# Spreading the conditioning row by DMA, taking both inverse roots in one chain, and splitting the first feature group into single blocks

## The chip, the cores and the metric

The kernel runs on one core of one Trainium2 chip. A core has a matrix engine (TensorE, PE in the tables), a vector engine (VectorE, DVE), a scalar engine (ScalarE, ACT), GpSimd (POOL) and SyncE (SP); each works through its own list of instructions strictly in order, and 16 DMA engines move data between HBM and the on-chip memory (SBUF). Matmul results land in a second on-chip memory, PSUM. The metric is the time of one execution in microseconds, as the device measures it.

## The reference

Two layers on 256 tokens of 1024 features. All is fp32. Cut to what matters here:

```
c_act = silu(c)                                   # c: one row of 1024
for l in range(2):
    mod = c_act @ w_ada[l] + b_ada[l]             # six vectors of 1024
    sh_a, sc_a, g_a, sh_f, sc_f, g_f = mod
    u = rmsnorm(x, attn_norm[l]) * (1 + sc_a) + sh_a
    y = token_mixer(u, w_in[l], ...)              # three branches, gates, w_out
    x = x + g_a * y
    hf = rmsnorm(x, ffn_norm[l]) * (1 + sc_f) + sh_f
    x = x + g_f * hier_moe(hf, ...)               # 16 experts, top 2 of one group
```

`u @ w_in` is the first matmul of a layer. Its input needs `rmsnorm(x)` and the first two vectors of `mod`, which need `silu(c)` and a third of `w_ada`.

## The kernel before

The change touches only the start of layer 0, up to the first three column chunks of `w_in` (called first, second and third chunk: 424, 512 and 512 columns).

**Conditioning row.** `c` (one row) is loaded into one partition; a matmul with a column of ones spreads it over 128 partitions into PSUM, in two halves of 512 (L266); ACT takes tanh (L267) and DVE makes `cb`, twice silu (L268).

**Norm.** `normed(t)` runs for the two blocks of 128 tokens: two squares with row sums on ACT (L439), then ten small DVE instructions (L440, L441 and the eight of `rsqrt`, L114 to L123), then two scalings on ACT into `xn` (L445).

**Groups of features.** The 1024 input features are eight blocks of 128, taken in four groups of two. For a group, DVE multiplies four half-megabyte pieces of `w_ada` with `cb` and sums along the row (`matvec`, L284, 128x1024 each); `modulation` adds bias and gain (L289, L292); ACT applies them to the transposed `xn` (L564, one per block) and rounds the result to the matmul type, `uh` (L565); DVE makes the rest, `ul` (L566). Each piece of `w_in` is split likewise: ACT makes `h` (L579), DVE makes `lo` (L580), both in one of four rotating buffers (`rs.get`, `rs.put`: rs_85 to rs_88). A buffer can be written again only when the matmuls that read it have ended. PE then multiplies `uh` by `h`, `ul` by `h` and `uh` by `lo` (`mm3`, L474 to L476; `second_chunk`, L503 to L505). Transposes of `xn` for the next group are issued a group ahead (`turned`, L546).

**Loads.** SP issues the list `loads` in order; up to eight transfers are in flight, and a transfer waits where its buffer is not yet free. Within a group the `w_ada` pieces stand ahead of the three `w_in` pieces. The order in which each engine runs its instructions is fixed when the program is built, by a scheduler: an instruction that waits holds all that is behind it on its engine.

Of the kernel before, what the change touches and what calls it, by code (L numbers as in the profile page):

```python
# [19 lines left out]
F32 = mybir.dt.float32  # L20
F32R = mybir.dt.float32r
I32 = mybir.dt.int32
AF = mybir.ActivationFunctionType
OP = mybir.AluOpType
# [3 lines left out]
L, D, S = 2, 1024, 256  # L28
EPS = 1e-6
# [42 lines left out]
def tile_block(ctx: ExitStack, tc: tile.TileContext, x_in, c_in, cst_in, sv_in, aux_in, wada_in, ws_in, out, depth=L):  # L72
    nc = tc.nc
    PE, DVE, ACT, POOL, SP = nc.tensor, nc.vector, nc.scalar, nc.gpsimd, nc.sync
# [4 lines left out]
    work = ctx.enter_context(tc.tile_pool(name="work", bufs=2))  # L79
# [17 lines left out]
    def mmt(name="mm"):  # L97
        return psum.tile([128, 512], F32, name=name)
# [3 lines left out]
    cb = persist.tile([128, D], F32, name="cb")  # L102
    x = fs.get().rearrange("p (t d) -> p t d", t=2)
    svs = [persist.tile([128, N_SV], F32, name=f"sv{l}") for l in range(depth)]
    ones = persist.tile([128, 128], F32, name="ones")
# [5 lines left out]
    def rsqrt(y, ms, n):  # L111

        t = work.tile([128, 64], F32, name="nt")[:, :n]
        DVE.tensor_scalar(y.bitcast(I32), ms.bitcast(I32), -0.5, 1597463007.0, op0=OP.mult, op1=OP.add)  # L114
        DVE.tensor_tensor(t, y, y, op=OP.mult)
        DVE.scalar_tensor_tensor(t, t, -0.5, ms, op0=OP.mult, op1=OP.mult)
        DVE.scalar_tensor_tensor(y, t, 1.5, y, op0=OP.add, op1=OP.mult)

        c = 0.375 ** 0.5
        DVE.tensor_tensor(t, y, y, op=OP.mult)  # L120
        DVE.scalar_tensor_tensor(t, t, c, ms, op0=OP.mult, op1=OP.mult)
        DVE.scalar_tensor_tensor(t, t, -1.25 / c, t, op0=OP.add, op1=OP.mult)
        DVE.scalar_tensor_tensor(y, t, 1.875, y, op0=OP.add, op1=OP.mult)  # L123
# [19 lines left out]
    halves = [slice(512 * hf, 512 * hf + 512) for hf in range(2)]  # L143
# [11 lines left out]
    for l in range(depth):  # L155
        w_order[l] += list(range(6, nd)) + [nd + i for i in expert_order]

    groups = [(0, 2), (2, 4), (4, 6), (6, 8)]
    for k0, k1 in groups:
        loads += [("b", 0, (i, k)) for k in range(k0, k1) for i in (k // 2, 4 + k // 2)]  # L160
        loads += [("p", 0, (2 * j + k0 // 4, k0 % 4, (k1 - 1) % 4 + 1)) for j in range(3)]
# [41 lines left out]
    def pump(most=len(loads)):  # L203

        for _ in range(most):
            if nxt[0] == len(loads):
                return
            kind, l, i = key = loads[nxt[0]]
            if kind == "u":
                if len(fs.free) < 2:  # L210
                    return
                t = [(fs, fs.get()), (fs, fs.get())]
                SP.dma_start(t[0][1][:, :1536], aux_in[l, :, :1536])
                SP.dma_start(t[1][1][:, :1024], aux_in[l, :, 1536:2560])
                SP.dma_start(wr, aux_in[l, :, 2560:])
            elif kind in "bp" and (i[1] % 2 if kind == "b" else i[1]):
                dst, src = part(kind, i)
                SP.dma_start(dst, src)
                loaded[key] = None
                nxt[0] += 1  # L220
                continue
            else:
                if wa.free:
                    t = (wa, wa.get())
                elif len(fs.free) > keep():
                    t = (fs, fs.get())
                elif lend[0] and rs.free and l == cur[0]:
                    t = (rs, rs.get(F32))
                else:
                    return  # L230
                if kind == "a":
                    SP.dma_start(t[1], wada_in[l, i])
                elif kind in "bp":
                    raws[kind, i[0]] = t
                    dst, src = part(kind, i)
                    SP.dma_start(dst, src)
                    t = None
                elif i < 2:
                    SP.dma_start(t[1][:, :4 * A0], ws_in[l, i, :, :4 * A0])
                else:  # L240
                    SP.dma_start(t[1], ws_in[l, i])
            loaded[key] = t
            nxt[0] += 1
# [8 lines left out]


    tmp_s = fs.get()
    tmp = tmp_s[:, :1024]
    crow = tmp_s[:1, 1024:]
    SP.dma_start(crow, c_in)
    SP.dma_start(x, x_in.rearrange("(t p) d -> p t d", p=128))
    pump(1)
    SP.dma_start(svs[0], sv_in[0])  # L260
    SP.dma_start(ident, cst_in[:, C_ID:C_ID + 128])
    pump()
    for hf in range(2):
        hs = slice(512 * hf, 512 * hf + 512)
        p = mmt("sm")
        PE.matmul(p, ones[:1], crow[:, hs], start=True, stop=True)  # L266
        ACT.activation(tmp[:, hs], p, AF.Tanh, scale=0.5)  # L267
        DVE.scalar_tensor_tensor(cb[:, hs], tmp[:, hs], 1.0, p, op0=OP.add, op1=OP.mult)  # L268

    fs.put(tmp_s)  # L270
    mods = [persist.tile([128, 48], F32, name=f"mod{l}") for l in range(depth)]
# [70 lines left out]
    def layer(l, tail):  # L342
# [85 lines left out]
        xn = xn_s.rearrange("p (t d) -> p t d", t=2)  # L428
        uf = uf_s.rearrange("p (k n) -> p k n", k=8)

        def normed(t):

            ss = work.tile([128, 2], F32, name="ss")
            ms = work.tile([128, 1], F32, name="msx")
            r = work.tile([128, 1], F32, name=f"rstd{t}")
            for hf, hs in enumerate(halves):
                if tail:
                    last_add(tail[0], t, hf)
                ACT.activation(xn[:, t, hs], x[:, t, hs], AF.Square, accum_out=ss[:, hf:hf + 1])  # L439
            DVE.tensor_tensor(ms, ss[:, 0:1], ss[:, 1:2], op=OP.add)  # L440
            DVE.tensor_scalar(ms, ms, 1.0 / D, EPS, op0=OP.mult, op1=OP.add)  # L441
            rsqrt(r, ms, 1)
            for hf, hs in enumerate(halves):
                if hf == 0 or not tail:
                    ACT.activation(xn[:, t, hs], x[:, t, hs], AF.Copy, scale=r)  # L445
                else:
                    DVE.tensor_scalar(xn[:, t, hs], x[:, t, hs], r, None, op0=OP.mult)
# [15 lines left out]
            return ops  # L463

        if not tail:
            for t in range(2):
                normed(t)

        def mm3(o, kb, nk, hv, lv, ah, al, t):
            ts = slice(128 * t, 128 * t + 128)  # L470
# [57 lines left out]
        else:  # L528
# [21 lines left out]
            for n_, (k0, k1) in enumerate(groups):  # L550
# [11 lines left out]
                p = nxt_p  # L562
# [6 lines left out]
                for j, do in enumerate((first_chunk, second_chunk, third_chunk)):  # L569
# [7 lines left out]
                    for k in range(k1 - k0):  # L577
                        r = raw[:, (k0 % 4 + k) * n:(k0 % 4 + k) * n + n]
# [21 lines left out]
        ss = work.tile([128, 2, 3], F32, name="ss_c", bufs=1)  # L600
# [8 lines left out]
        ms = work.tile([128, 4], F32, name="ms", bufs=1)  # L609
# [171 lines left out]
        for t in range(2):  # L781
            ts = slice(128 * t, 128 * t + 128)
            for src, dst, g in ((qc, qT, V_GQ), (kc, kT, V_GK)):
                for gg in range(2):
                    p = mmt("sm")[:96].rearrange("p (h n) -> p h n", h=4)
# [136 lines left out]
        for a in range(2):  # L922
# [13 lines left out]
            for bb in range(2):  # L936
                p = mmt("sm").rearrange("p (b n) -> p b n", b=2)
# [25 lines left out]
        for b, (yT_s, yT) in enumerate(((yaT_s, yaT), (ybT_s, ybT), (ycT_s, ycT))):  # L963
# [15 lines left out]
            if b == 1:  # L979
# [6 lines left out]
                p = mmt("sm")[:, :160]  # L986
# [3 lines left out]
            for hf in range(2):  # L990
                ps = dense(yT[:, 0], yT[:, 1], 4)
                hs = slice(512 * hf, 512 * hf + 512)
# [340 lines left out]
    def last_add(acc, t, hf):  # L1333

        hs = slice(512 * hf, 512 * hf + 512)
        DVE.tensor_tensor(x[:, t, hs], x[:, t, hs], acc[t][hf], op=OP.add)  # L1336
# [6 lines left out]
    for l in range(depth):  # L1343
        tail = layer(l, tail)
# [130 lines left out]
```

## Time and profile before

| what | value |
|---|---|
| median of 3 runs | 803.78 us (800.3 to 804.21) |
| the profiled execution | 806.04 us, span 804.3 us |
| PE busy | 760.3 us (95%) |
| DVE busy | 563.7 us (70%) |
| ACT busy | 386.0 us (48%) |
| DMA | 234.47 MB, mean 292 GB/s |

The profile is of one execution; the span runs from its first to its last instruction. Busy time of PE is modelled and includes overlap in its pipeline. Instants below are microseconds from the start of the span.

### The profile page before, as it was taken

The numbers are of one execution on the slowest core, as the hardware profiler recorded it, in microseconds if no ns is written. First come the engines' busy times: TensorE is split into PE (matmuls) and PEld (weight loads), VectorE is DVE, ScalarE is ACT, GpSimd is POOL, SyncE is SP. The second block draws the span as 40 slices with busy tenths as digits, with TensorE's granted clock in tenths as the row PEclk, the third lists the DMA queues.
The fourth block names the chain that finished last, engine by engine and source line by source line (L and its number), as shares of the span: only waits on it lengthen the run. The fifth ranks groups of instructions, "written<-read, shape, count | busy, mean of one in ns | idle before, by whom it ended". The sixth has DMA issues, their size and how long they took to land. (4 is left out here: it accounts for less than half of the span.)

```text
span 804.3 us, 12512 instructions
## 1 busy us (share of the span) xinstructions
PE 760.3 (95%) x4524; PEld 516.8 (64%) x4524; DVE 563.7 (70%) x1414; ACT 386.0 (48%) x851; POOL 30.0 (4%) x58
## 2 busy tenths in 40 slices
PE   4999999999999979999969999999999998999996
PEld 2885887878888854333349588888888876533332
DVE  6889978988899775323379998998757576633234
ACT  6467755664454533111167775576555543512111
POOL 0103000100000010000000400000000001000000
PEclk9999988999999989999989999999999999799999
DMA  8983654788989964999957367778885654499993
GB/s 338 406 343 116 250 211 157 262 309 330 384 302 426 383 247 171 423 421 420 420 211 262 114 253 261 238 262 288 330 326 201 246 202 154 167 420 421 420 422 143
DMA packets 36115, 234.47 MB, mean 292 GB/s; under 512 B 4017, under 2 KB 4689, under 8 KB 10450
## 3 DMA queue, kind: packets, MB, share of 16 engines
q1 hardware_dynamic: 35410, 231.52, 74.5%
q0 software_dynamic: 576, 2.10, 0.8%
q8 instruction: 37, 0.61, 0.3%
q14 instruction: 28, 0.23, 0.1%
q10 hardware_dynamic: 64, 0.02, 0.0%
HBM read 232.55 MB, written 1.06 MB: 290 GB/s over the span
## 5 line engine op out<-in xcount | busy, mean ns | idle before, releaser
L365 ACT ACTIVATE rs<-wa 128x512 fp32r<-128x512 f32 (+1 forms) x224 | 134.9, 633 | 90.1 <-PE mm L475 58.6
L474 PE MATMUL mm<-rs,rs 128*128 128x512 f32 (+1 forms) x432 | 172.1, 401 | 6.2 <-ACT rs L565 5.6
L365 DVE TENSOR_TENSOR rs<-wa,rs 128x512 fp32r<-128x512 f32 (+1 forms) x224 | 148.5, 683 | 39.5 <-ACT rs L365 26.7
L475 PE MATMUL mm<-rs,rs 128*128 128x512 f32 (+1 forms) x432 | 174.2, 404 | 0.4 <-DVE rs L462 0.3
L476 PE MATMUL mm<-rs,rs 128*128 128x512 f32 (+1 forms) x432 | 174.2, 404 | 0.0
L284 DVE SCALAR_TENSOR_TENSOR wa<-wa,cb 128x1024 f32<-128x1024 f32 x90 | 108.0, 1216 | 0.0
L474 PEld LDWEIGHTS mm<-rs,rs 128*128 128x128 f32 x432 | 82.2, 192 | 23.0 <-ACT rs L565 6.9
L475 PEld LDWEIGHTS mm<-rs,rs 128*128 128x128 f32 x432 | 82.7, 191 | 16.6 <-DVE rs L566 1.1
L476 PEld LDWEIGHTS mm<-rs,rs 128*128 128x128 f32 x432 | 83.1, 192 | 15.7 <-issue 1.3
L1210 DVE SCALAR_TENSOR_TENSOR th<-th,mm 128x256 f32<-128x256 f32 x16 | 6.7, 421 | 82.2 <-ACT th L1209 82.2
L1201 PE MATMUL mm<-fs,xs 128*32 128x512 f32 x384 | 58.7, 593 | 0.0
L1201 PE MATMUL mm<-wa,xs 128*32 128x512 f32 x320 | 54.0, 604 | 0.0
L1209 ACT ACTIVATE th<-mm 128x256 f32<-128x256 f32 x16 | 6.1, 383 | 95.8 <-PE mm L1201 95.8
L109 ACT ACTIVATE fs<-fs 128x512 fp32r<-128x512 f32 x32 | 20.1, 629 | 56.3 <-DVE fs L1234 56.3
L1201 PE MATMUL mm<-rs,xs 128*32 128x512 f32 x320 | 42.8, 594 | 0.0
L109 DVE TENSOR_TENSOR fs<-fs,fs 128x512 fp32r<-128x512 f32 x32 | 22.1, 692 | 22.8 <-ACT fs L109 22.8
L474 PE MATMUL mm<-rs,xs 128*128 128x512 f32 x96 | 37.6, 392 | 0.0
L476 PE MATMUL mm<-rs,xs 128*128 128x512 f32 x96 | 37.5, 391 | 0.0
L475 PE MATMUL mm<-rs,xs 128*128 128x512 f32 x96 | 37.4, 390 | 0.0
L1234 DVE TENSOR_TENSOR fs<-mm,fs 128x512 f32<-128x512 f32 x32 | 22.0, 687 | 20.9 <-PE mm L1232 20.9
L365 ACT ACTIVATE rs<-fs 128x512 fp32r<-128x512 f32 x40 | 23.8, 627 | 22.9 <-PE mm L475 14.8
L1201 PEld LDWEIGHTS mm<-fs,xs 128*32 128x32 f32 x384 | 15.9, 110 | 29.0 <-issue 28.4
(333 smaller groups left out, 1276.8 us busy)
## 6 DMA issues: line engine op xcount, KB each, us to landing
wa<-in_ws_dram SPq DMA_DIRECT2D x83, 1024.0 KB, 7.1
fs<-in_ws_dram SPq DMA_DIRECT2D x47, 1024.0 KB, 10.3
wa<-in_wada_dram SPq DMA_DIRECT2D x40, 1024.0 KB, 5.3
rs<-in_ws_dram SPq DMA_DIRECT2D x30, 1024.0 KB, 12.4
wa<-in_wada_dram SPq DMA_DIRECT2D x10, 512.0 KB, 9.9
wa<-in_ws_dram SPq DMA_DIRECT2D x6, 512.0 KB, 9.2
fs<-in_wada_dram SPq DMA_DIRECT2D x6, 512.0 KB, 10.0
fs<-row POOLq DMA_DIRECT2D x4, 512.0 KB, 7.8
```

The source lines that it names most:

```text
L109: return ACT.activation(h, src, AF.Copy), DVE.tensor_tensor(l, src, h.bitcast(F32), op=OP.subtract)
L284: DVE.scalar_tensor_tensor(w, w, 0.5, cb, op0=OP.mult, op1=OP.mult, accum_out=mods[l][:, 2 * i + j:2 * i + j + 1])
L365: pinned(ACT.activation(h[:, cs_], r[:, cs_], AF.Copy), DVE.tensor_tensor(lo[:, cs_], r[:, cs_], h[:, cs_].bitcast(F32), op=OP.subtract))
L474: PE.matmul(o, ah[:, kb + k, ts], hv[:, k], start=st, stop=False)
L475: PE.matmul(o, al[:, kb + k, ts], hv[:, k], start=False, stop=False)
L476: PE.matmul(o, ah[:, kb + k, ts], lv[:, k], start=False, stop=en)
L1201: queued(PE.matmul(pgu[64 * t + 32 * i:64 * t + 32 * i + 32], xg[kb // 2][:, kb % 2, 2 * q + i, t], wv[i][:, k], start=kb == 0, stop=kb == 7))
L1209: ACT.activation(th, pgu[:, :256], AF.Tanh, scale=0.5)
L1210: DVE.scalar_tensor_tensor(th, th, 1.0, pgu[:, :256], op0=OP.add, op1=OP.mult)
L1234: DVE.tensor_tensor(y, py[hf], rows[:, 1, hs], op=OP.mult)
```

## The change

Three edits. `c` is spread by its load: the transfer itself reads the 4 KB row once for each of 128 partitions, from ACT's queue, and tanh and `cb` are one instruction each on 128x1024. The norm of both token blocks is made at once: the ten small DVE instructions work on two columns, and the four scalings follow all of them. The first group of two feature blocks becomes two groups of one block, so that there are five groups.

```diff
-    groups = [(0, 2), (2, 4), (4, 6), (6, 8)]
+    groups = [(0, 1), (1, 2), (2, 4), (4, 6), (6, 8)]
...
-    tmp = tmp_s[:, :1024]
-    crow = tmp_s[:1, 1024:]
-    SP.dma_start(crow, c_in)
+    tmp, crow = tmp_s[:, :1024], tmp_s[:, 1024:]
+    ACT.dma_start(crow, c_in.to_broadcast([128, 1024]))
     SP.dma_start(x, x_in.rearrange("(t p) d -> p t d", p=128))
...
-    for hf in range(2):
-        hs = slice(512 * hf, 512 * hf + 512)
-        p = mmt("sm")
-        PE.matmul(p, ones[:1], crow[:, hs], start=True, stop=True)
-        ACT.activation(tmp[:, hs], p, AF.Tanh, scale=0.5)
-        DVE.scalar_tensor_tensor(cb[:, hs], tmp[:, hs], 1.0, p, op0=OP.add, op1=OP.mult)
+    ACT.activation(tmp, crow, AF.Tanh, scale=0.5)
+    DVE.scalar_tensor_tensor(cb, tmp, 1.0, crow, op0=OP.add, op1=OP.mult)
...
         if not tail:
+            ss = work.tile([128, 2, 2], F32, name="ss0", bufs=1)
+            ms, r = work.tile([128, 2], F32, name="msx0", bufs=1), work.tile([128, 2], F32, name="rs0", bufs=1)
             for t in range(2):
-                normed(t)
+                for hf, hs in enumerate(halves):
+                    ACT.activation(xn[:, t, hs], x[:, t, hs], AF.Square, accum_out=ss[:, t, hf:hf + 1])
+            DVE.tensor_tensor(ms, ss[:, :, 0], ss[:, :, 1], op=OP.add)
+            DVE.tensor_scalar(ms, ms, 1.0 / D, EPS, op0=OP.mult, op1=OP.add)
+            rsqrt(r, ms, 2)
+            for hf, hs in enumerate(halves):
+                for t in range(2):
+                    ACT.activation(xn[:, t, hs], x[:, t, hs], AF.Copy, scale=r[:, t:t + 1])
```

In the changed file the lines stand four or five off: `matvec` is L279, L289 and L292 are L284 and L287, L445 is L471, L564 to L566 are L568 to L570, L579 and L580 are L583 and L584, and L474 to L476 are L478 to L480. From the third group on (blocks 2 and 3) every engine has the same instructions in the same order as before; what differs lies ahead of it.

On DVE before, this is the piece from the second product with `w_ada` (wa_67, `cb`) to the first product of the next group (fs_73); the root of the second token block ends right behind the former.

```order
L284 SCALAR_TENSOR_TENSOR wa_67,mod_122<-wa_67,cb 128x1024
L123 SCALAR_TENSOR_TENSOR rstd_144<-nt,rstd_144 128x1
L284 SCALAR_TENSOR_TENSOR wa_66,mod_122<-wa_66,cb 128x1024
L289 TENSOR_TENSOR mod_122<-mod_122,sv_91 128x2
L284 SCALAR_TENSOR_TENSOR wa_67,mod_122<-wa_67,cb 128x1024
L289 TENSOR_TENSOR mod_122<-mod_122,sv_91 128x2
L292 SCALAR_TENSOR_TENSOR mod_122<-mod_122,sv_91 128x2
L580 TENSOR_TENSOR rs_85<-wa_68,rs_85 128x424 x2
L566 TENSOR_TENSOR rs_84<-fs_76,rs_83 128x512
L580 TENSOR_TENSOR rs_86<-wa_69,rs_86 128x512 x2
L580 TENSOR_TENSOR rs_87<-fs_72,rs_87 128x512 x2
L284 SCALAR_TENSOR_TENSOR fs_73,mod_122<-fs_73,cb 128x1024
```

On DVE after, the same place: the second half of the root (nt, rs_123) stands behind the second product and behind one split.

```order
L279 SCALAR_TENSOR_TENSOR wa_67,mod_119<-wa_67,cb 128x1024
L120 TENSOR_TENSOR nt<-rs_123 128x2
L584 TENSOR_TENSOR rs_85<-wa_68,rs_85 128x424
L121 SCALAR_TENSOR_TENSOR nt<-nt,msx_122 128x2
L284 TENSOR_TENSOR mod_119<-mod_119,sv_91 128x1
L122 SCALAR_TENSOR_TENSOR nt<-nt 128x2
L287 SCALAR_TENSOR_TENSOR mod_119<-mod_119,sv_91 128x1
L123 SCALAR_TENSOR_TENSOR rs_123<-nt,rs_123 128x2
L584 TENSOR_TENSOR rs_86<-wa_69,rs_86 128x512
```

On ACT after, from the scalings of `xn` (fs_75) to the second group's first piece of the third chunk: four buffers take six pieces, so the fifth, marked by its wait for PE, writes rs_85 again.

```order
L471 ACTIVATE fs_75<-fs_70,rs_123 128x512 [waits Activation_49]
L568 ACTIVATE fs_76<-sm,mod_119 128x256 [waits PE_49]
L583 ACTIVATE rs_87<-fs_72 128x512 [waits DMAHW0_49]
L569 ACTIVATE rs_83<-fs_76 128x256 [waits Activation_49]
L583 ACTIVATE rs_88<-wa_68 128x424 [waits DMAHW3_49]
L583 ACTIVATE rs_85<-wa_69 128x512 [waits DMAHW4_49,PE_49]
L568 ACTIVATE fs_76<-sm,mod_119 128x256 [waits DVE_49]
L569 ACTIVATE rs_83<-fs_76 128x256 [waits Activation_49]
L583 ACTIVATE rs_86<-fs_72 128x512 [waits DMAHW5_49,PE_49]
```

On PE after, the start of the first group: the matmuls that read rs_85 end with the eighth of these rows, behind two each of the other chunks.

```order
L550 MATMUL sm<-cst,fs_75 128x128 x4
L478 MATMUL mm<-rs_85,rs_83 128x424 x2
L507 MATMUL mm<-rs_83,rs_86 128x256 x2
L478 MATMUL sm<-rs_87,rs_83 128x512 x2
L479 MATMUL mm<-rs_85,rs_84 128x424
L480 MATMUL mm<-rs_85,rs_83 128x424
L479 MATMUL mm<-rs_85,rs_84 128x424
L480 MATMUL mm<-rs_85,rs_83 128x424
L508 MATMUL mm<-rs_84,rs_86 128x256
```

Before, all six matmuls of a block and chunk stood together, and the three chunks of a group followed one another.

## Rows read from the trace of the kernel before

**Rows 1.** The page: span and instructions.

```profile
span 804.3 us, 12512 instructions
```

**Rows 2.** Windows of 5 us: length, busy time of PE, PEld, DVE, ACT, POOL, clock, DMA.

```profile
20.00:25.00 5.00, 5.00 (x29) 4.89 (x28) 4.97 (x9) 0.56 (x1) 0.00 (x0) 1.00 1.05 410
```

**Rows 3.** Timeline, DVE: start, duration, line; products and ends of modulation by group.

```profile
15.04 0.16 DVE L292 SCALAR_TENSOR_TENSOR mod<-mod,sv 128x2 f32<-128x2 f32 x1
...
22.61 1.22 DVE L284 SCALAR_TENSOR_TENSOR fs<-fs,cb 128x1024 f32<-128x1024 f32 x1
...
25.41 0.16 DVE L292 SCALAR_TENSOR_TENSOR mod<-mod,sv 128x2 f32<-128x2 f32 x1
...
46.19 0.16 DVE L292 SCALAR_TENSOR_TENSOR mod<-mod,sv 128x2 f32<-128x2 f32 x1
```

**Rows 4.** Timeline, the start: loads of c and x, the scalings, the first product.

```profile
0.75 0.35 SPq L257 DMA_DIRECT2D fs<-in_c_dram  x1
...
1.16 0.41 SPq L258 DMA_DIRECT2D fs<-in_x_dram  x1
...
11.14 2.62 ACT L445 ACTIVATE fs<-fs,rstd 128x512 f32<-128x512 f32 x4 [1.86 <-DVE nt L122]
...
17.33 1.07 PE L474 MATMUL mm<-rs,rs 128*128 128x424 f32 x2 [2.59 <-ACT rs L565]
```

**Rows 5.** One line's transfers in a short window: x; second w_ada piece; next group's first.

```profile
DMA to landing us min/median/max: 4.9/4.9/4.9
...
L236 SPq DMA_DIRECT2D wa<-in_wada_dram x1: 440/440/440, 3.2 to 3.2; - x1
...
DMA to landing us min/median/max: 7.1/7.1/7.1
...
L236 SPq DMA_DIRECT2D fs<-in_wada_dram x1: 738/738/738, 7.8 to 7.8; - x1
...
DMA to landing us min/median/max: 10.0/10.0/10.0
```

**Rows 6.** Timeline, DVE: the next group's first product with w_ada.

```profile
20.32 1.22 DVE L284 SCALAR_TENSOR_TENSOR fs<-fs,cb 128x1024 f32<-128x1024 f32 x1
```

**Rows 7.** Groups by line and form, first 50 us: count, busy, mean ns, idle before.

```profile
L579 ACT ACTIVATE rs<-wa 128x512 fp32r<-128x512 f32 x12 | 6.7, 622 | 0.0
L564 ACT ACTIVATE fs<-sm,mod 128x256 f32<-128x256 f32 x7 | 3.6, 559 | 8.4 <-DVE mod L292 8.4
...
L284 DVE SCALAR_TENSOR_TENSOR wa<-wa,cb 128x1024 f32<-128x1024 f32 x10 | 12.0, 1220 | 0.0
...
L580 DVE TENSOR_TENSOR rs<-wa,rs 128x512 fp32r<-128x512 f32 x10 | 6.3, 685 | 0.0
...
L580 DVE TENSOR_TENSOR rs<-wa,rs 128x424 fp32r<-128x424 f32 x4 | 2.4, 599 | 2.1 <-ACT rs L579 2.1
```

**Rows 8.** Timeline, PE: neighbouring matmuls in the first group.

```profile
19.28 0.56 PE L475 MATMUL mm<-rs,rs 128*128 128x424 f32 x1
...
19.64 0.56 PE L476 MATMUL mm<-rs,rs 128*128 128x424 f32 x1
...
22.40 0.41 PE L503 MATMUL mm<-rs,rs 128*128 128x256 f32 x1
...
22.61 0.41 PE L504 MATMUL mm<-rs,rs 128*128 128x256 f32 x1
```

**Rows 9.** Timeline, PE: first matmuls of the last two groups, with the idle time before.

```profile
38.11 0.65 PE L474 MATMUL mm<-rs,rs 128*128 128x424 f32 x2 [1.25 <-ACT rs L565]
...
48.42 0.66 PE L474 MATMUL mm<-rs,rs 128*128 128x424 f32 x2 [1.76 <-ACT rs L565]
```

**Rows 10.** Windows of 1 us: PE busy, granted clock, DMA share, GB/s.

```profile
50.00:51.00 1.00, 1.00 (x5) 0.62 1.04 434
...
53.00:54.00 1.00, 1.00 (x8) 0.68 0.98 410
```

**Rows 11.** The page's DMA queues: packets, MB, share of 16 engines.

```profile
q0 software_dynamic: 576, 2.10, 0.8%
```

## The prediction

> **What bounds the kernel now.** Since the order on every engine is the same from the third group on, I asked only two things of the profile: when does the work of the third group's blocks (2 and 3) begin, before and after; and does a shift there reach the end. First the page for the span [rows 1], then the windows of 5 us: from 20 to 25 us DVE is busy 4.97 of 5.00 and the DMA moves 410 GB/s [rows 2]. So two limits lie close together here. Then the timeline of DVE: modulation of the four groups ends with L292 at 15.04, 25.41, once more between, and 46.19 [rows 3], a period of 20.78 / 2 = 10.4 us, set by DVE's own list: of products with `w_ada` at 1.22 us and splits at 0.60 to 0.69 [rows 7] it has some ten microseconds per group. The loads are ahead of it: the next group's first `w_ada` piece, issued at 7.8, has landed 10.0 later, at 17.8 [rows 5], and is used at 20.32 [rows 6]: 2.5 us of slack. PE is behind DVE in the late groups: it stands idle 1.25 and 1.76 us before the first matmul of the third and fourth [rows 9], which ACT's `uh` releases. From 48.42 on it has work without a gap to the end of the stage. So each microsecond by which DVE passes a group later starts the last group later, and PE's list behind it has nothing that shortens. I take it that the rest of the kernel keeps a shift: loads there begin when buffers come free, and these shift too.
>
> **The row by DMA.** It removes two small matmuls and a second tanh and a second `cb` at the start; none of them is on the path, since the first product with `w_ada` waits for its own piece, too. It adds 128 x 4 KB = 0.524 MB ahead of that piece: 1.28 us at 410 GB/s [rows 2]. SP no longer issues `c`, so `x` is issued at 0.75 in place of 1.16 [rows 4]: 0.41 back. All pieces land 0.87 later, the second `w_ada` piece at 3.2 + 7.1 + 0.87 = 11.2 [rows 5]. For the later groups the slack of 2.5 hides it; for the first it does not. Bounds: +0 if the start-up holds the extra bytes, +1.3 without the head start. A spread row of the same size on GpSimd's queue took 0.8% of 16 engines' span for 2.10 MB [rows 11], 2.10 / (0.008 x 804) = 0.33 MB per us, so at worst 1.6 us for 0.524 MB.
>
> When does `c` land? `x` took 4.9 us from issue [rows 5]. With `c` first it is there at about 4.4, behind `x` at 0.75 + 4.9 + 1.28 = 6.9. Tanh and `cb` on 1024 columns take about 1.2 each (DVE's product of that shape takes 1.22 [rows 7]), so `cb` is ready between 6.8 and 9.4, and the first product cannot start ahead of its piece at about 8.3. I take the middle, which costs nothing; the late end pushes the second product by 0.5. The Trainium skill (DMA: Bandwidth & Descriptors, Queues, rings and completion order) says that a DMA engine takes turns between the queues it has work for; by that, `c` lands when as much of `x` has moved, near 5.7, and the sum has nothing from it, where the late end would make it 3.7.
>
> **Both roots in one chain.** Ten small DVE instructions go. But the list now puts the second half of the root behind the second product, and one split of 424 columns between. That product waits for the landing at 11.2 and ends at 12.4; the split takes 0.60 [rows 7], six small ones, 0.16 each [rows 3] and about half of it overlapped, another 0.5: the root is done at 13.5. Before, the first scaling ran at 11.14 [rows 4] and `xn` was ready long before modulation ended at 15.04. Now four scalings, 2.62 us [rows 4], end at 16.1, later than modulation, and are the path.
>
> **Single blocks.** Modulation of block 0 is ready at 13.4, two products earlier than before, but nobody can use it until 16.1. Then ACT has L564 (0.56), a split that is ahead of `uh` in its list (0.62) [rows 7], and `uh` on 256 columns, at most 0.62, taken as 0.5, less 0.1 of overlap: the first matmul runs at 17.7, against 17.33 [rows 4].
>
> Each one-block group takes three of the four rotating buffers, so the second piece of the second group writes rs_85, which the first chunk of the first group is read from. PE runs there at its lower level of 1.2 GHz: 0.36 us per 424 columns and 0.21 per 256 [rows 8], so 0.43 per 512. Ahead of the buffer's release stand two each of 424, 256 and 512 columns and four more of 424: 0.72 + 0.42 + 0.86 + 1.44, and 0.2 for the last one's end: 3.6, so it is free at 21.3. ACT's split follows (0.62), to 21.9. ACT is held meanwhile and with it the second group's modulated input; DVE, whose next instruction is the other half of that split, has been through with all ahead of it since about 19.6. This wait of 2.3 us is what the change adds. Behind it DVE still has: split (0.60), product (1.15), a rest of 256 columns (0.36), split (0.60), second product (1.15), with small overlaps taken off the rows' durations: the third product of the third group starts at 21.9 + 3.9 = 25.8. Before it started at 22.61 [rows 3]. **The sum is +3.2 us.** The profiled execution took 806.04 us, 1.7 more than its span; 809.2 is the sum there, and against the median of the runs, 803.78, it is 807.0.
>
> Bounds of the chain: with PE at its higher level the release comes 1.5 earlier, +1.7; with loads that are not late 0.87 less, +2.3; with `c` late 0.5 more, +3.7. The Trainium skill (TensorE: Matmul & The Clock Gate, Part 1) says that the throttled state is the default and that activity releases it, which speaks against cutting up the first group: the first buffer's release is always paid at the low level. The rows have it so: 0.36 us per 424 columns is the lower level.
>
> **Rivals.**
> *DVE never waits.* If the buffer is free in time, DVE's list alone decides: from the landing at 11.2 some 11.1 us of work to the third product, 22.3, 0.3 better than before; 1.2 better with loads in time. Ten small instructions fewer and PE's earlier start speak for it, PE at 1.2 GHz against it. 802.6 to 803.5. It decides once the rs_85 matmuls end before 19.6.
> *The clock.* In the last group PE fell to the lower level, from 50.2 to 53.6 by the windows [rows 10], after the 1.76 us of idleness; the gap of 1.25 had no such sequel [rows 9]. A fall of 3.4 us costs 1.7 where PE is the bound, nothing where PE waits anyway. After the change two gaps near 1.8 are left; if the fall comes one group earlier the last group is spared: +1.5, 805.3. Faster than the kernel before needs both rivals: 803.5 - 1.7 = 801.8, with loads in time 800.9.
> *The spread is slow.* Reading one row 128 times could run below the 0.33 MB per us of [rows 11]. The second product waits for bytes queued behind it, so each microsecond more is a microsecond on the path; from 0.8 on, the kernel is over 0.5% slower. At 0.17 MB per us, half, it is 1.8 more: 808.8. For it speaks only that no such load stands in this trace at the start.
> *It does nothing.* The stage's end would be held by loads: no, these have 2.5 us of slack and DVE is full.
>
> **How the numbers follow.** Runs of this kernel spread over 3.9 us, so 0.5% (4.0 us) is what can be told from no change. Chances: the wait with the same clock 0.55 (807.0, by its bounds 805.5 to 807.5); with the fall moved 0.2 (805.3); DVE never waits, alone or with the clock, 0.1 (800.9 to 803.5); a slow spread or another fall on top 0.15 (808 to 811). The likeliest gives 807.0. The range 802.5 to 809.5 takes in all but the ends of the last two. Over 807.8 lies the last case and, by the runs' own spread, a fifth of the first: 0.27. Under 799.8 only the spread of runs reaches: 0.05. Within: 0.68.
>
> **What would show it.** In the changed profile: the second product with `w_ada` at about 11.2 behind a DMA; scalings from 13.5 in one run to 16.1; the first product at 17.7; ACT's split into rs_85 waiting for PE until 21.3, and DVE idle about 2 us before its other half; modulation of blocks 2 and 3 ending at 28.6 in place of 25.41, and then the old period of 10.4. I am wrong if PE's first chunk is through before 19.6, if the root is done ahead of the second product, or if the shift at 28.6 is not found again at the last group's first matmul, near 51.6.

## The result, and the profile after

| | before | after |
|---|---|---|
| median | 803.87 us (800.13 to 806.54, 16 runs) | 809.17 us (803.8 to 812.79, 16 runs) |
| ratio, 95% interval | | 1.0068 (1.0046 to 1.009) |
| profiled execution | 806.04 us, span 804.3 | 809.19 us, span 807.4 |

The changed kernel is slower by 0.7%. The forecast was 807.0 us within 802.5 to 809.5, with "no measurable change" as the likeliest and "slower" at 0.27. By the prediction's own mark of 0.5% this comparison shows the less likely case, and its median lies only 0.3 us under the upper end of the range. The path was the one forecast; the two largest differences from the sum are a start that is later than costed, and clock falls that differ from one run to the next.

The page after, against [rows 1]: the span is 3.1 us longer with 12 instructions fewer.

```profile
span 807.4 us, 12500 instructions
```

The timeline of DVE after (start, duration, line, operation; in brackets the idle time before it and what ended it) answers to [rows 3, 4, 6]. The idle 2.46 us is the new wait; the end of the modulation of blocks 2 and 3 (L287) stands at 28.89, where it was at 25.41.

```profile
9.59 1.23 DVE L279 SCALAR_TENSOR_TENSOR wa<-wa,cb 128x1024 f32<-128x1024 f32 x1 [0.95 <-DMA wa<-in_wada_dram]
...
11.88 1.22 DVE L279 SCALAR_TENSOR_TENSOR wa<-wa,cb 128x1024 f32<-128x1024 f32 x1
...
13.99 0.16 DVE L123 SCALAR_TENSOR_TENSOR rs<-nt,rs 128x2 f32<-128x2 f32 x1
...
18.12 0.43 DVE L570 TENSOR_TENSOR rs<-fs,rs 128x256 fp32r<-128x256 f32 x1 [0.88 <-ACT rs L569]
...
22.26 0.69 DVE L584 TENSOR_TENSOR rs<-wa,rs 128x512 fp32r<-128x512 f32 x1 [2.46 <-ACT rs L583]
...
26.10 1.22 DVE L279 SCALAR_TENSOR_TENSOR fs<-fs,cb 128x1024 f32<-128x1024 f32 x1
...
28.89 0.16 DVE L287 SCALAR_TENSOR_TENSOR mod<-mod,sv 128x2 f32<-128x2 f32 x1
```

The same stretch on ACT: `c` is there at 6.32 and `x` at 8.19, the scalings run from 14.25, and ACT stands for 3.06 us before the split that writes the first buffer again, until PE's L479 lets it go.

```profile
6.32 1.06 ACT L262 ACTIVATE fs<-fs 128x1024 f32<-128x1024 f32 x1 [3.82 <-DMA fs<-in_c_dram]
8.19 0.63 ACT L465 ACTIVATE fs<-fs 128x512 f32<-128x512 f32 x1 [0.81 <-DMA fs<-in_x_dram]
...
14.25 2.56 ACT L471 ACTIVATE fs<-fs,rs 128x512 f32<-128x512 f32 x4 [1.07 <-DVE rs L123]
...
21.59 0.63 ACT L583 ACTIVATE rs<-wa 128x512 fp32r<-128x512 f32 x1 [3.06 <-PE mm L479]
```

On PE the first matmul stands at 18.14, and that of the last group at 52.07, 3.65 later than in [rows 9]; the idle 1.77 us ahead of the latter is the same as before, so PE passes the delay on unshortened.

```profile
18.14 1.07 PE L478 MATMUL mm<-rs,rs 128*128 128x424 f32 x2 [1.81 <-ACT rs L569]
...
52.07 0.66 PE L478 MATMUL mm<-rs,rs 128*128 128x424 f32 x2 [1.77 <-ACT rs L569]
```

### The profile page after: what moved, and what is told of

Same layout as the page of the kernel before. It is cut to its first block, busy times and chain, and to the rows that moved or that the text cites. A ratio compares the mean times of both kernels' runs of the same rounds, so it can differ in the third digit from the quotient of the medians.

```text
span 807.4 us, 12500 instructions
## 1 busy us (share of the span) xinstructions
PE 757.0 (94%) x4520; PEld 516.0 (64%) x4520; DVE 563.2 (70%) x1407; ACT 386.6 (48%) x851; POOL 33.9 (4%) x58
## 5 line engine op out<-in xcount | busy, mean ns | idle before, releaser
L478 PE MATMUL mm<-rs,rs 128*128 128x512 f32 (+1 forms) x432 | 172.2, 402 | 5.2 <-ACT rs L569 4.6
L479 PE MATMUL mm<-rs,rs 128*128 128x512 f32 (+1 forms) x432 | 175.1, 406 | 0.4 <-DVE rs L457 0.3
L480 PE MATMUL mm<-rs,rs 128*128 128x512 f32 (+1 forms) x432 | 174.5, 405 | 0.0
L279 DVE SCALAR_TENSOR_TENSOR wa<-wa,cb 128x1024 f32<-128x1024 f32 x90 | 108.3, 1219 | 1.0 <-DMA wa<-in_wada_dram 1.0
L478 PEld LDWEIGHTS mm<-rs,rs 128*128 128x128 f32 x432 | 82.0, 191 | 22.2 <-ACT rs L569 6.1
L479 PEld LDWEIGHTS mm<-rs,rs 128*128 128x128 f32 x432 | 83.3, 193 | 16.4 <-DVE rs L570 0.9
L480 PEld LDWEIGHTS mm<-rs,rs 128*128 128x128 f32 x432 | 83.6, 193 | 15.9 <-issue 1.4
L478 PE MATMUL mm<-rs,xs 128*128 128x512 f32 x96 | 37.6, 391 | 0.0
L480 PE MATMUL mm<-rs,xs 128*128 128x512 f32 x96 | 37.5, 391 | 0.0
L479 PE MATMUL mm<-rs,xs 128*128 128x512 f32 x96 | 37.4, 390 | 0.0
```

Source lines behind the costliest of these rows:

```text
L279: DVE.scalar_tensor_tensor(w, w, 0.5, cb, op0=OP.mult, op1=OP.mult, accum_out=mods[l][:, 2 * i + j:2 * i + j + 1])
L478: PE.matmul(o, ah[:, kb + k, ts], hv[:, k], start=st, stop=False)
L479: PE.matmul(o, al[:, kb + k, ts], hv[:, k], start=False, stop=False)
L480: PE.matmul(o, ah[:, kb + k, ts], lv[:, k], start=False, stop=en)
```

## The experiments

Two theories at first. A: single blocks make ACT, and with it DVE, wait for the first buffer, and this is most of the loss. B: the spread row's bytes and the root behind the second product are the loss, and the wait only covers for them. Later runs have an A and a B of their own, which stand in the expectation of each. Besides the times I compare one instant in each trace, called **E**: the start of the instruction that ends the modulation of blocks 2 and 3. It is 25.41 before and 28.89 after. The start of equal programs differs by 0.2 to 0.4 us from trace to trace (the unaltered changed kernel had E at 28.89 and 28.50), so differences below that are not read. The column "1 + shift / 804" is the ratio that the shift alone would give.

| kernel | first product | E | shift of E | 1 + shift / 804 | measured ratio (95%) |
|---|---|---|---|---|---|
| changed | 9.59 | 28.89 | +3.48 | 1.0043 | 1.0068 (1.0046 to 1.009) |
| changed, again | 9.21 | 28.50 | +3.09 | 1.0038 | 1.0044 (1.0025 to 1.0063) |
| changed, half buffers | 9.26 | 26.04 | +0.63 | 1.0008 | 1.0003 (0.9978 to 1.0027) |
| changed, four groups | 9.48 | 27.66 | +2.25 | 1.0028 | 1.0015 (0.9985 to 1.0044) |
| changed, row by matmul | 7.55 | 27.70 | +2.29 | 1.0028 | 1.0032 (1.0009 to 1.0054) |
| before + single blocks | 8.19 | 28.02 | +2.61 | 1.0032 | 1.0016 (0.9995 to 1.0036) |
| before + spread row | 9.18 | 26.34 | +0.93 | 1.0012 | 1.0022 (0.9998 to 1.0046) |
| before + one chain | 7.62 | 25.41 | 0.00 | 1.0000 | 0.9997 (0.9973 to 1.002) |
| before + single blocks, half buffers | 7.98 | 25.36 | -0.05 | 0.9999 | 0.9987 (0.9959 to 1.0014) |

Six of these nine intervals hold 1.0 too, so the ratios alone cannot tell a shift of 2 us from none; the readings below rest on the traces.

**Half buffers** (the changed kernel; `shared` holds the first group's three buffers).

```diff
+            shared = []
...
-                    w_s = rs.get()
-                    hv = w_s[:, :(k1 - k0) * n].rearrange("p (k n) -> p k n", n=n)
-                    lv = w_s[:, 1024:1024 + (k1 - k0) * n].rearrange("p (k n) -> p k n", n=n)
+                    w_s = shared[j] if n_ == 1 else rs.get()
+                    if n_ == 0:
+                        shared.append(w_s)
+                    o_ = 512 if n_ == 1 else 0
+                    hv = w_s[:, o_:o_ + (k1 - k0) * n].rearrange("p (k n) -> p k n", n=n)
+                    lv = w_s[:, 1024 + o_:1024 + o_ + (k1 - k0) * n].rearrange("p (k n) -> p k n", n=n)
...
-                    rs.put(w_s)
+                    if n_ > 0:
+                        rs.put(w_s)
```

> The changed kernel, but the second single block is split into the other halves of the three buffers of the first, so that ACT's split into rs_85 has no matmul to wait for. Theory A (the wait for the buffer is most of the loss): ACT's split comes at about 18.6 in place of 21.59, DVE's other half at 19.8 in place of 22.26, and all behind it moves by 2.4 us: modulation of blocks 2 and 3 ends at 26.4 (changed kernel 28.89), the first matmul of the last group is at 49.6 (52.07), and the time is 2.4 us below the changed kernel's, about 806.7. Theory B (late loads and the late root are the loss, and the wait only covers for them): something else ends last at that place, modulation ends at 28 or later, and the time stays near 809.

The wait is gone and nothing of its size takes its place. DVE's split comes at 19.39 behind the work ahead of it, and E moves by 2.85, of which 0.33 is the earlier first product in this trace:

```profile
18.81 0.59 DVE L588 TENSOR_TENSOR rs<-wa,rs 128x424 fp32r<-128x424 f32 x1
...
19.39 0.68 DVE L588 TENSOR_TENSOR rs<-wa,rs 128x512 fp32r<-128x512 f32 x1
...
26.04 0.16 DVE L287 SCALAR_TENSOR_TENSOR mod<-mod,sv 128x2 f32<-128x2 f32 x1
```

The median falls to that of the kernel before; the trace has E 0.63 later than there. Theory A holds for the changed kernel.

**Four groups** (the changed kernel with `groups` as before).

```diff
-    groups = [(0, 1), (1, 2), (2, 4), (4, 6), (6, 8)]
+    groups = [(0, 2), (2, 4), (4, 6), (6, 8)]
```

> The changed kernel with the four groups of two blocks that the kernel before has; the spread row and the one chain of roots stay. Theory A: no split waits for a buffer that matmuls still read; what is left is the late first piece of w_ada and the root behind the second product, so modulation of blocks 2 and 3 ends between 25.8 and 26.9 (kernel before 25.41, changed kernel 28.89), and the time is 0.5 to 1.5 us over the kernel before's. Theory B (late loads and root are the loss): modulation ends at 28 or later, and the time is near 807 to 809.

Neither: E is 27.66, between the two, with no buffer to wait for. In this program's order DVE has the end of the root behind the third product, not behind the second as in the changed kernel. The scalings end at 17.34, ACT's `uf` (the modulated input, L568) and second split follow, and DVE waits 2.39 us for that split.

```profile
14.52 0.16 DVE L123 SCALAR_TENSOR_TENSOR rs<-nt,rs 128x2 f32<-128x2 f32 x1
...
18.72 0.60 DVE L584 TENSOR_TENSOR rs<-wa,rs 128x424 fp32r<-128x424 f32 x1 [2.39 <-ACT rs L583]
...
27.66 0.16 DVE L287 SCALAR_TENSOR_TENSOR mod<-mod,sv 128x2 f32<-128x2 f32 x1
```

So in this order the late root, which theory A had counted too low, costs 1.3 us beyond the spread's 0.93 (below). With the five groups it doesn't: the half buffers have the same spread and the same chain, no wait for a buffer, and E only 0.63 late.

**Row by matmul** (the changed kernel with the load and the spread of `c` as before).

```diff
...
-    ACT.dma_start(crow, c_in.to_broadcast([128, 1024]))
+    SP.dma_start(crow, c_in)
...
+        PE.matmul(p, ones[:1], crow[:, hs], start=True, stop=True)
```

> The changed kernel with the conditioning row spread by matmul as in the kernel before; the single blocks and the one chain of roots stay. The first product is back at about 8.2 (9.59 in the changed kernel). Theory A: PE starts about 1.2 us earlier and the buffer is free that much earlier, but DVE still waits for ACT's split, 1 to 2.5 us; modulation of blocks 2 and 3 ends between 27.0 and 27.7, and the time is 1.2 to 1.9 us below the changed kernel's. Theory B (the spread row is the loss): modulation ends at 26 or earlier, with no wait on DVE, and the time is within 0.6 us of the kernel before's.

E is 27.70, the upper end of theory A. DVE still waits for ACT: 0.82 us behind the scalings, then 1.01 and 0.58 for splits that wait for a buffer. PE's first matmul is at 16.21 instead of 18.14, so the first wait for a buffer is shorter (1.01 for 2.46), and a second one, for the next buffer, appears. Theory B is out.

```profile
20.32 0.69 DVE L589 TENSOR_TENSOR rs<-wa,rs 128x512 fp32r<-128x512 f32 x1 [1.01 <-ACT rs L588]
...
27.70 0.16 DVE L292 SCALAR_TENSOR_TENSOR mod<-mod,sv 128x2 f32<-128x2 f32 x1
```

**Single blocks alone** (the kernel before with the five groups).

```diff
-    groups = [(0, 2), (2, 4), (4, 6), (6, 8)]
+    groups = [(0, 1), (1, 2), (2, 4), (4, 6), (6, 8)]
```

> The kernel before with the single blocks alone; the row by matmul and the two roots stay. Theory A (the buffer wait comes from the single blocks themselves): PE's first matmul is near 15.3, 2 us earlier than in the kernel before, the first buffer is free near 18.9, ACT's split ends near 19.5, and DVE waits about 1 us for it; modulation of blocks 2 and 3 ends between 26 and 27, and the time is 0.6 to 1.6 us over the kernel before's. Theory B (with scalings in time PE is early enough that DVE never waits): modulation ends at 25.5 or earlier, and the time is the kernel before's or less.

Theory A was right in kind and too small: DVE waits twice on account of a buffer, 0.71 and 1.56 us, the second time for the next buffer, which the second chunk's matmuls still read.

```profile
19.67 0.69 DVE L580 TENSOR_TENSOR rs<-wa,rs 128x512 fp32r<-128x512 f32 x1 [0.71 <-ACT rs L579]
...
21.99 0.69 DVE L580 TENSOR_TENSOR rs<-fs,rs 128x512 fp32r<-128x512 f32 x1 [1.56 <-ACT rs L579]
```

**The changed kernel again, and the other two parts alone.** The first is unaltered; the others are the kernel before with one part each of the diff ahead of the prediction: its lines on `crow`, or its lines on `ss`, `ms` and `r`.

```diff
-    SP.dma_start(crow, c_in)
+    ACT.dma_start(crow, c_in.to_broadcast([128, 1024]))
```

```diff
-                normed(t)
...
+            rsqrt(r, ms, 2)
```

> The changed kernel once more, unaltered. If the shift of 3.5 us that its trace has from the end of the modulation of blocks 2 and 3 on is all that the change costs, the ratio to the kernel before is 1.0044 within the measurement's own uncertainty (1.002 to 1.0065); if the change also costs about 2 us somewhere later (more or longer stretches at TensorE's lower clock), the ratio is again 1.0065 or more.

> The kernel before with the spread row alone. The first product with w_ada is at 9.3 to 9.6 (kernel before 8.18), as in the three kernels with the spread so far; no split waits for a matmul. Theory A (the spread is a plain delay of the first pieces): modulation of blocks 2 and 3 ends 0.8 to 1.4 us later than before, at 26.2 to 26.8, and the time is up by as much, a ratio of 1.001 to 1.002. Theory B (it is the late x, by way of the roots and ACT's scalings, that DVE then waits for): the scalings end after 16 and DVE waits about 2 us for ACT's split, modulation ends at 27.4 or later, and the time is up by 2 us or more.

> The kernel before with the one chain of roots alone; row by matmul, groups of two blocks. Theory A (with x in time the chain is nearly free, since modulation ends last): the last instruction of the root is behind the second product, near 12.1, the scalings run from 12.3 to 14.9, and modulation of blocks 2 and 3 ends at 25.3 to 25.8 (kernel before 25.41); the time is that of the kernel before within 0.5 us. Theory B (the later scalings hold ACT and DVE): a wait of 1 us or more on DVE ahead of its first split, modulation at 26.4 or later, the time up by 1 us or more.

The repeat gave 1.0044, what a shift of 3.5 us makes; its interval ends at 1.0063, so that a further 1.5 us is not ruled out by it alone. The spread row alone delays E by 0.93, as theory A had it, with a wait of only 0.80 on DVE; the one chain alone by nothing, since with `x` in time its scalings (12.39 to 14.95) end before the modulation. The two ends of modulation in the kernel with the spread row alone, 0.87 and 0.93 later than in [rows 3], and the wait between them:

```profile
15.91 0.16 DVE L287 SCALAR_TENSOR_TENSOR mod<-mod,sv 128x2 f32<-128x2 f32 x1
...
17.72 0.60 DVE L575 TENSOR_TENSOR rs<-wa,rs 128x424 fp32r<-128x424 f32 x1 [0.80 <-ACT rs L574]
...
26.34 0.16 DVE L287 SCALAR_TENSOR_TENSOR mod<-mod,sv 128x2 f32<-128x2 f32 x1
```

Alone the three parts cost 0.93, 0.00 and 2.61, together 3.54, and the change costs 3.48. The agreement of the sum is no proof that the parts are independent. Spread and chain as a pair cost 2.25 with four groups and 0.63 with five groups and half buffers: what they cost goes by the place that the root's end gets in DVE's order.

**Single blocks with half buffers** (the kernel before with both edits, that of `groups` and that of `shared`).

> The kernel before with the single blocks, and with the second block split into the other halves of the first one's buffers; row by matmul, two roots. Theory A (DVE's own list is the bound, so single blocks bring nothing even where no split waits for a matmul): modulation of blocks 2 and 3 ends at 25.5 to 26.0, which is the 28.02 of the single blocks alone less its two waits of 0.71 and 1.56, and the time is that of the kernel before to 0.5 us more. Theory B (PE's start, 2 us earlier, pays once the wait is gone): modulation ends at 25.0 or earlier, and the time is lower by 0.5 us or more.

E is 25.36 with a first product 0.2 earlier than before, 25.56 with that put back: theory A by the trace, while the ratio's interval holds both. PE's first matmul is at 15.34 instead of 17.33, and E gains nothing from the two microseconds, since DVE, not PE, sets the pace up to the last group.

```profile
15.34 1.08 PE L474 MATMUL mm<-rs,rs 128*128 128x424 f32 x2 [1.26 <-ACT rs L566]
```

**Towards a faster kernel.** In the kernel before DVE waits about 1 us in each group for ACT's second split behind `uf` (1.07, 1.07, 0.89 and 0.98). This is the second of them, in the kernel before:

```profile
27.16 0.60 DVE L580 TENSOR_TENSOR rs<-wa,rs 128x424 fp32r<-128x424 f32 x1 [1.07 <-ACT rs L579]
```

Three forms of the kernel before put splits earlier; `early_split` holds the body of the split, taken out of the loop over the chunks.

```diff
+                early = [early_split(j) for j in range(1)]
                 for c in (0, 8):
                     modulation(0, c + k0, c + k1)
...
                 for j, do in enumerate((first_chunk, second_chunk, third_chunk)):
+                    w_s, hv, lv, h_, raw_p, raw = early[j] if j < 1 else early_split(j)
```

> The kernel before, with the split of each group's first chunk put ahead of the modulation in the order of the code, so that ACT does both halves of it while it waits for the modulation, and DVE has three splits to do while ACT writes uf and uh. In the kernel before DVE waits about 1.0 us for ACT at this place in each of the four groups. Theory A (that wait is on the path): modulation of blocks 2 and 3 ends at 24.3 to 24.6 (25.41), that of blocks 6 and 7 at 43 to 44 (46.19), the first matmul of the last group at 45.3 to 46.8 (48.42), and the time is 1.5 to 3 us lower, a ratio of 0.996 to 0.998. Theory B (the loads, which move 410 GB/s there, are as full as DVE): the wait for ACT turns into waits for pieces of w_ada, modulation of blocks 6 and 7 ends at 45.5 or later, and the time is the same.

With the first and second chunk early:

```diff
-                early = [early_split(j) for j in range(1)]
+                early = [early_split(j) for j in range(2)]
```

> The kernel before with the splits of the first and second chunk of each group ahead of the modulation in the order of the code. With the first chunk's alone DVE still waits 0.6 us per group for ACT's second split of 512 columns; here ACT does it ahead of uh. Theory A (what is left of the wait is still on the path): DVE has no wait for ACT in the groups, modulation of blocks 6 and 7 ends at 42.8 to 43.8 (45.02 with the first chunk's alone), uh comes 0.6 later behind it, the first matmul of the last group is at 45.8 to 46.8 (47.33), and the time is 0.5 to 1.5 us below that kernel's, a ratio of 0.994 to 0.996 to the kernel before. Theory B (the loads or PE are the bound by now): waits for pieces of w_ada or PE without a gap ahead of the last group, its first matmul stays at 47.2 or later, and the ratio is 0.9965 or more.

With half of the second chunk early, and `uf` behind it on ACT:

```diff
+                early_split(0, (0, 1))
+                early_split(1, (0,))
...
+                    behind_of(o_, cut_ops[1, 0])
```

> The kernel before, with the first chunk's two splits and the second chunk's first one ahead of the modulation in the code, and ACT's uf held behind them, so that DVE has the work of three splits ready when a modulation ends. Theory A (the 0.64 us for which DVE still waits for ACT in each group of the two kernels with earlier splits is on the path): DVE has no wait for ACT in the groups; modulation of blocks 2 and 3 ends near 24.4 (24.98 with the first chunk's splits alone), that of blocks 6 and 7 near 43.2 (45.02), the first matmul of the last group is near 45.5 (47.33), and the ratio to the kernel before is 0.993 to 0.996. Theory B (the loads set the pace from here): pieces of w_ada come up as what DVE waits for in the later groups, modulation of blocks 6 and 7 ends at 44.5 or later, and the ratio stays at 0.9965 or above.

And the first of them once more:

> The kernel before with the first chunk's splits ahead of the modulation, once more, unaltered. Its trace has the last group's first matmul 1.1 us earlier (47.33 for 48.42), while its ratio was 0.9965 (0.9945 to 0.9986), 2.8 us. If the shift of 1.1 us is all that it gives, the ratio is 0.9986 within the measurement's uncertainty (0.9965 to 1.0005); if it also gives something later, the ratio is again 0.9965 or less.

| kernel | E | end of modulation, blocks 6 and 7 | last group's first matmul | measured ratio (95%) |
|---|---|---|---|---|
| before | 25.41 | 46.19 | 48.42 | |
| first chunk early | 24.98 | 45.02 | 47.33 | 0.9965 (0.9945 to 0.9986) |
| first and second chunk early | 24.77 | 44.81 | 47.64 | 0.9965 (0.9939 to 0.9991) |
| first chunk and half the second, `uf` behind them | 24.26 | 44.62 | 46.93 | 0.9992 (0.9966 to 1.0019) |
| first chunk early, again | 24.77 | 44.81 | 47.11 | 1.0016 (0.9989 to 1.0043) |

With the first chunk early DVE still waits for ACT's split of 512 columns, so the gain is 0.4 per group and not the 1.0 expected.

```profile
26.82 0.69 DVE L571 TENSOR_TENSOR rs<-wa,rs 128x512 fp32r<-128x512 f32 x1 [0.64 <-ACT rs L570]
```

Taking the second chunk along leaves that wait where it was (0.64): both theories had left out that `uf` still stands ahead of it on ACT (`uf` at 25.02, the split at 25.94). Only the third form takes it away in the first two groups. In its third group a load comes up, as theory B of it said, though with a piece of `w_in` and not of `w_ada`:

```profile
35.22 0.63 ACT L574 ACTIVATE rs<-wa 128x512 fp32r<-128x512 f32 x1 [2.17 <-DMA wa<-in_ws_dram]
```

The third form is 0.72 ahead of the first at E and only 0.40 at the end of the modulation of blocks 6 and 7, where two more waits removed should have given more. In that trace the loads move 405 to 417 GB/s from 25 to 45 us; that they are the next bound is what this one wait suggests, and no run here went further.

The first form gave 0.9965 and, unaltered, 1.0016. Its last group starts 1.1 us earlier, which is 0.9986. A gain of that size fits both intervals to within 0.0003; a faster kernel is not shown. Set side by side at the same mean clock (as told below, under the total), its runs are 1.0 and 0.8 us shorter than those of the kernel before, which fits 1.1, but that way of counting is off by as much elsewhere. The second form's interval, too, ends under 1.0, but there is only one comparison of it, and the two of the first form show how little one says here.

## Why the prediction came out as it did

**The bound, and that a shift reaches the end: right.** From 28.89 the changed kernel's groups follow at 39.46 and 49.84, periods of 10.57 and 10.38 where 10.4 was taken, and the last group's first matmul is 3.65 late, against 3.2 predicted. In eight of the nine comparisons of the first table the ratio that the shift of E gives lies within the measured interval; for the changed kernel's first 1.0068 it lies 0.0003 outside, for its repeat inside.

**The row by DMA: the effect right, the first product mis-sized.** I had the first product at 8.3, as the bytes ahead of its piece end; it came at 9.59, and at 9.2 to 9.5 in the other kernels with the spread. The bytes themselves went as counted. This is the DMA's rate after, in slices of 0.25 us from 0 to 10:

```profile
GB/s 0 0 0 0 0 0 0 147 115 115 66 147 246 328 328 311 377 426 393 393 393 410 442 410 442 410 393 377 360 410 426 331 328 415 402 366 365 394 340 375
```

Summed up, 1.57 MB, as much as `c` and `x` have, had moved at 6.75, 2.1 MB (with the first piece) at 8.2, and 2.6 MB at 9.5. But `x` was used at 8.19 and the piece at 9.59, both after a wait for DMA: by then half a megabyte more had moved than stands up to them in the lists, so bytes from behind them had moved beside them. A constant delay after the last byte doesn't account for all of it: in the kernel before `x` landed at 6.06 (1.16 + 4.9 by [rows 4, 5]), and by the same count 1.3 MB had moved then, only a quarter of a megabyte too many. The Trainium skill (DMA: Bandwidth & Descriptors, Queues, rings and completion order) says that an engine takes turns between the queues it has work for; `c` at 6.3, behind 5.7 by that rule and inside my 4.4 to 6.9, agrees with it in kind. For `x` and the piece the rule gives nothing, since they stand in one queue, SP's; why bytes behind them moved beside them is open. The step of mine that failed is the landing counted from the bytes ahead alone, 8.3 for 9.59. The second product was then not held by its landing at 11.2, as I had it, but ran at 11.88 without a wait for DMA, behind the first half of the root. That is 0.7 late. Against the kernel before (11.02) it is 0.86, the 0.87 that I had put down for the bytes, but by another mechanism: this agreement is luck. The rival "the spread is slow" is not borne out: alone the spread costs 0.93.

**The roots: right for this order.** Root done predicted 13.5, measured 14.15; scalings to 16.1, measured 16.81; first matmul 17.7, measured 18.14. That the place behind the second product would decide was right; that with `x` in time the chain is free was shown only by running it alone.

**The single blocks: right.** ACT's split predicted at 21.3, measured 21.59; DVE idle 2.3, measured 2.46; third product of the third group 25.8 and 26.10; modulation 28.6 and 28.89. Each instant is 0.3 late; the 0.7 at the scalings' end shrank to 0.4 at the first matmul (ACT's three instructions ahead of it took 1.33 for 1.6) and to 0.3 at the release (3.45 for 3.6).

**The rivals.** "DVE never waits" would have had the buffer free before 19.6; it came 2 us later. The half buffers made that case, and the rival's price was wrong: the third product was to come at 22.3, 0.3 better than before, and came at 23.25, 0.64 worse. The second product ran at 11.55 for 11.2, and DVE stood 0.88 us for ACT's `uh`, which the rival's list had left out. "The clock falls a group earlier and spares the last" is not borne out either: in the profiled execution the clock fell in the third group and again in the last, as the windows of 1 us show (after the windows' length come busy times of five engines, then the granted clock), and in the repeat only in the last. Of the two gaps near 1.8 that I expected ahead of the late groups only one is there, 1.77; the other is 0.71.

```profile
33.00:34.00 1.00, 1.00 (x5) 0.93 (x4) 1.00 (x3) 0.66 (x2) 0.00 (x0) 0.50 1.04 396
...
53.00:54.00 1.00, 1.00 (x4) 0.93 (x5) 1.00 (x3) 1.00 (x3) 0.00 (x0) 0.50 0.91 385
```

**The total.** 807.0 was 803.8 + 3.2. The shift in the trace is 3.5; from the medians of the first comparison it is 5.3, of the second 3.8. The two comparisons of one and the same kernel lie 1.5 us apart. What lies between them goes with the clock. The mean granted clock is on record for each run of the changed kernel and for 127 of the kernel before, from the later comparisons, so runs at one clock can be set side by side. At 0.979 six runs of the changed kernel have a mean of 807.0 us, and 24 of the kernel before 802.7. Over all clocks that both kernels have, the changed kernel is 3.4 us longer in the first comparison (13 of its 16 runs) and 4.1 in the repeat (12 runs), where the traces have shifts of 3.5 and 3.1. For the other kernels of the table this way of counting comes within 1.2 us of the shift, so it is no finer than that. Whether the change itself makes the clock fall more often, or the first 16 runs met more falls by chance, is open. That 809.17 still lay inside the range is luck to the extent of those 1.8 us, and so is the agreement of the profiled execution (809.19) with the sum (809.2): its mean clock was 0.972, and 0.975 in the one before.

## What to carry to other kernels

Cutting the first tile so that the matrix engine starts sooner pays only if that engine sets the pace there. Here, with the row by matmul, two roots and half buffers, it started 2 us sooner for nothing. In the changed kernel the smaller pieces used up the rotating buffers while PE still ran at its low level. Before splitting a group, count how many buffers the pieces take and find the instant at which the first is free. Before putting a row that spreads over partitions ahead of other loads, ask which loads share the engines with it: here the first piece behind it landed 1.3 us later than the bytes ahead of it said. Where changes are under 1%, compare one instant in the traces, and runs at the same mean clock, besides the medians.

## What the runs showed that was not expected

**Where the clock falls differed between two executions of one kernel, and this outweighs the change.** The same changed kernel, twice: in windows of 50 us the granted clock is 1.00 and 0.90 between 100 and 150 us, and 0.90 in both between 500 and 550 (1.00 there in the kernel before). The first two rows are from the first trace, the other two from the repeat.

```profile
100.00:150.00 50.00, 49.95 (x288) 40.79 (x286) 45.77 (x135) 34.28 (x89) 2.24 (x1) 1.00 0.54 195
500.00:550.00 50.00, 50.00 (x238) 39.72 (x236) 44.58 (x134) 31.50 (x84) 0.00 (x0) 0.90 0.61 216
```

```profile
100.00:150.00 50.00, 49.98 (x255) 40.23 (x255) 41.38 (x126) 30.00 (x82) 0.03 (x1) 0.90 0.47 169
500.00:550.00 50.00, 49.94 (x235) 39.27 (x235) 44.32 (x133) 28.44 (x70) 0.00 (x0) 0.90 0.65 231
```

A tenth of 50 us is 5 us lost where PE is the bound, and the repeat, which is 0.4 us ahead at E, ends 4.5 us behind (span 811.9 for 807.4); smaller differences in other windows go both ways. Over the first 16 runs of the changed kernel the time goes with the mean clock, from 803.8 us at 0.980 to 811.79 and 812.42 at 0.968. What sets the place of these falls is open.

**The low level in the first group doesn't show in the clock's column.** It reads 1.00 in each window of 1 us from 17 to 27, while matmuls of 256 columns stand 0.21 us apart up to 22.1 and 0.12 behind it. The level was read from the spacing:

```profile
21.71 0.41 PE L508 MATMUL mm<-rs,rs 128*128 128x256 f32 x1
21.92 0.38 PE L509 MATMUL mm<-rs,rs 128*128 128x256 f32 x1
22.14 0.29 PE L507 MATMUL mm<-rs,rs 128*128 128x256 f32 x1
22.26 0.28 PE L508 MATMUL mm<-rs,rs 128*128 128x256 f32 x1
```

The Trainium skill (TensorE: Matmul & The Clock Gate, Part 1) has the low level as the default that activity ends, and the spacing agrees. But the instant at which the spacing halves differs: 3.3 us after the group's first matmul in the kernel with the row by matmul, 4.0 in the changed one, 6.1 in that with four groups. Whether a buffer is released at the low or the high level could therefore not be had from counting matmuls: DVE waited for the second buffer not at all in the changed kernel, and 0.58 and 1.56 us in those with the row by matmul and with single blocks alone.

**Two products of DVE took longer beside GpSimd's work.** While POOL's L666 ran (34.23 to 39.38), two of DVE's products took 1.32 and 1.31 us in place of 1.22; this is the 0.2 us by which that period is longer than the next. A third product under the same work, at 38.00, took 1.22, so that GpSimd is the cause is not shown.
